# Grouped-query q norm folded into the exponentials' scale, with scalar maxima, first PSUM banks and the final scale changed

## The chip, the cores and the metric

The kernel runs on one core of a Trainium2 chip. The metric is the device time of one execution in microseconds (us), lower is better. The kernel before takes 1393.04 us, the median of three runs (1392.54 to 1395.71). Engine names as in the profile: PE is TensorE, DVE VectorE, ACT ScalarE, POOL GpSimd, SP SyncE, which issues the DMAs.

## The reference

Two layers of an encoder trunk over 512 tokens of 1024 features, f32, batch 1:

```
x = x + W_out [ NA-heads(h) || GQA-heads(h) ],   h = rms_norm(x) and one input projection
x = x + memory_cross_attention(rms_norm(x), rms_norm(mem))      4 heads of 128, 256 memory tokens
x = x + conv_ffn(rms_norm(x))                                   SwiGLU with a depthwise conv
return rms_norm(x)
```

The eight neighbourhood (NA) heads look at a window of the token grid. The grouped-query (GQA) part has 8 query heads and 2 key/value heads of 64, and this is what the change is mostly about:

```
g_q = apply_axial_rope(rms_norm(g_q, q_norm), cos, sin)      norm over each head's 64 numbers
g_k = apply_axial_rope(rms_norm(g_k, k_norm), cos, sin)
sc  = einsum('bqkgd,bskd->bkgqs', q, k) * HEAD_DIM ** -0.5
p   = softmax(sc);  o = p @ v
```

The rms of a query head is one number for a row of sc. So it can multiply q before the scores, or stand as a scale on the row of scores when its maximum is found and its exponentials are taken.

## The kernel before, in words

Activations lie transposed (features on partitions, 512 tokens along the row). Products in f32 precision are made from pairs of fp32r numbers, a high and a low part: each product is three matmuls (hi hi, hi lo, lo hi), so every tensor that PE reads has to be split: ACT casts (hi) and DVE or POOL subtracts (lo). Weights are loaded by SP, cast on ACT (L265) and subtracted on POOL (L266).

PE runs its instructions in the order of the program, and so does SP. The instructions of ACT, DVE and POOL are put in an order by a scheduler, by data and by priorities: `with behind(n)` makes instructions yield to others by n places, or go ahead where n is negative. `late(n, fn)` puts work off until n more units of PE's filler have been issued, so that its inputs are ready when PE comes to it.

PSUM has eight banks, in three pools: four "mm" (`ps_mm`, projections and attention values), two "sc" (`ps_s`, scores) and two "tr" (`ps_t`, transposes and small sums). A bank that is asked for again has to be read out first.

The stages of a layer. In attention the scores, softmax, transposes and values of 8 NA units and then of 16 GQA units of 128 queries (a pair of heads each) are woven step by step, and each step is filled up with other PE work worth some 2300 to 3000 ns, drawn from `attn_fill`. That is one sequence: the NA projections (`project_first` in layer 0, with the first three units interleaved; `project_qk`; `project_v`), the GQA projections in the order k, 0, 1, v, 2, 3 (`gqa_project`; 0 to 3 are q, two heads each), the NA part of the output projection (`out_na`), memory keys and values, and `close_rows`, the GQA part of the output projection. `attn_fill.step(N_FIRST ...)` runs the first units of it ahead of the weave. When the sequence has nothing ready, a step is not filled. Memory attention and the FFN follow.

The GQA path, `gqa_rope` (L834): q or k comes out of the projection in an mm bank `pm`. ACT writes xs, the bank by gain (L840), and its square sq (L841), DVE writes cc, the bank by gain and cosine (L842). Then pm is free. One unit later, `swap`: SP moves xs by 32 partitions into xr with four DMAs; PE sums sq over each head with the matrix `pairs`, into a tr bank; DVE makes v, mean square plus eps (L852, L855). Then `rotate`: POOL raises v to the power -1/2 (L862), copies it wide (L863), multiplies xr by the sine (L864) and adds cc (L865). Then `norm`: four PE matmuls with the identity turn the wide rows into a new mm bank (L77 `mm<-ident,t`). Then `split`: DVE multiplies (L875) and `split_q` (ACT L682, DVE L684) or `split_k` (ACT L664 and L666, DVE L668 and L670) makes the pairs. GQA's v goes through a transpose (`turn`).

The scores, `gqa_scores`: DVE takes each row's negative maximum out of the sc bank (L900), ACT the exponential with it as bias and the sum (L902); `gqa_normalise` takes 1/sum (L908) and multiplies (POOL L479). `normalise` (L478) is the tensor_scalar at L479, on DVE or POOL. NA's parts: scores L739, exponentials L745, one normalisation on ACT (L757), the others on POOL (L479), halves joined by L789 and L790, and the finished part split by `split_out` (ACT L499, POOL L500), which `out_na` waits for. `split_psum` is the general split (ACT L472, DVE L473).

Memory attention's scores, `mem_scores`: one DVE reduce for two query blocks (L1076), the product of the two maxima by 1/rms (L1077), two exponentials with 1/rms as scale (L1081). At the end of the kernel `scale` multiplies each half row of x by the final gain on ACT (L1241), beside the last residual adds (L1271) and the final norm (L400, L403, L413, L1249, L1251).

Line numbers in the text are those of the kernel before.

Of the kernel before, what the change touches and what calls it, by code (L numbers as in the profile page):

```python
# [10 lines left out]
F32 = mybir.dt.float32  # L11
F32R = mybir.dt.float32r
AF = mybir.ActivationFunctionType
ALU = mybir.AluOpType
# [4 lines left out]
P = 128  # L19
S = 512  # L20
# [29 lines left out]
MEM_FILL = [1, 1, 2, 2, 1, 3, 1, 3, 1, 3, 1]  # L50
N_ROWS = 3
MEM_STEPS = [0, 0, 1, 0, 1, 1, 1, 1, 1, 1, 1] + [0] * 9
W_BEHIND, N_RAW, N_W, AHEAD, AHEAD_HELD, N_WARM, N_LATE, N_FIRST = 45, 2, 4, 2, 5, 8, 4, 3


class InOrder:
# [117 lines left out]
def encoder_kernel(ctx: ExitStack, tc: tile.TileContext, t: dict, out: bass.AP):  # L174
# [29 lines left out]
    def rtile(shape, dt=F32R):  # L204
        return rpool.tile([P, *shape], dt, tag="r", name=nm("r"), padded_shape=[P, *pad(shape)])
# [63 lines left out]
    def get_w(key, ahead=AHEAD):  # L269
        n = done[0]  # L270
        assert plan[n][0] == key, (plan[n][0], key)
        ahead = n + 1 + ahead
        while ahead < min(len(plan), n + 1 + AHEAD_HELD) and plan[ahead][4][1:] == "r":
            ahead += 1
        while len(ready) < min(len(plan), ahead):
            while len(raws) < min(len(plan), len(ready) + N_RAW):
                emit_raw()
            emit_split()
        while len(raws) < min(len(plan), len(ready) + N_RAW):
            emit_raw()  # L280
        done[0] += 1
        w = ready[n]
        ready[n] = None
        return w
# [245 lines left out]

    mem_rstd = cpool.tile([P, MB], F32, name="mem_rstd")
    mem_rep = cpool.tile([P, MEMN], F32, name="mem_rep")

    def mem_stat():
        raw = load_mem()
# [53 lines left out]
    for l in range(DEPTH):  # L589
# [11 lines left out]
        def project_first():  # L601

            w, pms = {}, {}
            for u, k0, k1 in ((0, 0, 2), (1, 0, 2), (0, 2, 4), (1, 2, 4), (2, 0, 4), (0, 4, 6),
                              (1, 4, 6), (2, 4, 6), (0, 6, 8), (1, 6, 8), (2, 6, 8)):
                if u not in w:
                    w[u], pms[u] = get_w(NA_ORDER[u]), ps_mm()
                if (u, k0) == (0, 0):

                    for k in range(2):  # L610
                        PE.matmul(pms[u], w[u][0][:, k], xg[k][0], start=k == 0, stop=False)
                        PE.matmul(pms[u], w[u][0][:, k], xg[k][1], start=False, stop=False)
# [12 lines left out]

            late(1, evict)
            yield
# [2 lines left out]

        def project_qk(n, p):
            w = get_w((n, p))
            pm = ps_mm()
            gemm_T(pm, w, xg, range(0, 4), 0, KC - 1)
            yield
            gemm_T(pm, w, xg, range(4, 8), 0, KC - 1)
            if (n, p) == ("q", 0):
                mix.stat()
                held.append(pm)
            elif (n, p) == ("k", 0):  # L640
                mix.spread()
# [192 lines left out]

        def gqa_rope(g, pm):

            gain = qkg[:, l, 0:1] if g != "k" else qkg[:, l, 1:2]
            xs, sq, cc = tmp(), tmp(), tmp()
            with behind(-20):
                ACT.activation(xs, pm, AF.Copy, scale=gain)  # L840
                ACT.activation(sq, pm, AF.Square)  # L841
                DVE.scalar_tensor_tensor(cc, pm, gain, gtab[0][:, 0], op0=ALU.mult, op1=ALU.mult)  # L842

            def swap():
                xr = tmp()
                for i in range(4):
                    SP.dma_start(xr[32 * i : 32 * i + 32], xs[32 * (i ^ 1) : 32 * (i ^ 1) + 32])
                pv = ps_t()
                for b in range(NB):
                    PE.matmul(pv[:, 2 * b : 2 * b + 2], sq[:, b * P : (b + 1) * P], pairs, start=True, stop=True)  # L850
                v = small(2 * NB)
                DVE.tensor_tensor(v.rearrange("p (b j) -> p b j", j=2), pv[:, 0 : 2 * NB].rearrange("p (b j) -> p b j", j=2),  # L852
                                  r2[0].unsqueeze(2).to_broadcast([P, NB, 2]), op=ALU.mult)

                DVE.tensor_scalar(v, v, *((1.0 / HD, EPS) if g == "k" else (1.0, EPS * HD)), op0=ALU.mult, op1=ALU.add)  # L855
# [12 lines left out]
            def norm(xr, rows):  # L868
# [3 lines left out]
                late(1, lambda: split(xr, pr))  # L872

            def split(xr, pr):
                DVE.tensor_mul(pr, xr, pr)  # L875
                if g == "k":
                    gk.extend(rtile((2, S)) for _ in range(2))
                    split_k(pr, gk, False)
                else:
                    gq[g] = rtile((2, S))  # L880
                    split_q(pr, gq[g])

            late(1, swap)


        ga, gpt = {}, {}

        def gqa_scores(u):
            i, b = divmod(u, NB)
            qs = slice(b * P, b * P + P)  # L890
            assert gq[i] is not None and gk and gvt
            sc = [ps_s() for _ in range(2)]
            for j in range(2):
                for part in range(2):
                    PE.matmul(sc[j], gq[i][:, j, qs], gk[j][:, part], start=part == 0, stop=part == 1)
            nmx, sums = small(2), small(2)
            es = []
            for j in range(2):
                c = slice(j, j + 1)
                DVE.tensor_reduce(nmx[:, c], sc[j], axis=AX.X, op=ALU.max, negate=True)  # L900
                e = tmp()
                ACT.activation(e, sc[j], AF.Exp, bias=nmx[:, c], accum_out=sums[:, c])  # L902
                es.append(e)
            ga[u] = es, sums

# [114 lines left out]
        if l > 0:  # L1020
# [48 lines left out]
        def mem_scores(u):  # L1069
            h, bp = divmod(u, 2)  # L1070
            sc = ps_s().rearrange("p (i n) -> p i n", i=2)
            for i in range(2):
                qs = slice((2 * bp + i) * P, (2 * bp + i + 1) * P)
                mm3(sc[:, i, :], *(v[:, qs] for v in mqs[h]), *memk[h], True, True)
            nmx, sums = small(2), small(2)
            DVE.tensor_reduce(nmx, sc, axis=AX.X, op=ALU.max, negate=True)  # L1076
            DVE.tensor_mul(nmx, nmx, mq.rstd[:, 2 * bp : 2 * bp + 2])  # L1077
# [154 lines left out]
        def down_last(g):  # L1232
# [144 lines left out]
```

## Time and profile before

| | |
|---|---|
| median of three runs | 1393.04 us |
| the profiled execution | 1393.77 us |
| its span in the trace | 1392.0 us |
| mean granted clock of PE in it | 0.994 |
| instructions in the trace | 19198 |
| read from HBM, written | 125.00 MB, 2.10 MB |
| mean DMA rate | 91 GB/s over the span |

How to read it. The rows of the next section are from the page of the profile and from answers of its trace. A row in order of time has start, duration, engine, line, operation, out<-in, partitions x elements and type, and in brackets how long the engine was idle before it and what ended that. A group row has, after the bar, the busy time of all in us, the mean of one in ns, and the idle time before them. Rows of stretches have start:end, length, busy us (and count) of PE, of its weight load PEld, of DVE, ACT and POOL, then the mean granted clock, the DMA share and GB/s. A PE row's duration overlaps the next row's start, so the time that a matmul costs is read from start to start. A short group of several instructions is one row, with xN.

### The profile page before, as it was taken

Reading aid. Unit: us, or ns where it says so; the run is one execution under the profiler, and the core shown is the slowest. Engines: PE = TensorE matmul, PEld = TensorE weight load, DVE = VectorE, ACT = ScalarE, POOL = GpSimd, SP = SyncE. Lnnn points to the kernel's source line nnn. Section 1 sums busy time; section 2 is a strip of 40 time slices with the busy share of each in tenths; the row PEclk is TensorE's granted clock in tenths of the full one; section 3 lists DMA queues with packets and bytes.
Section 4 is the critical chain, followed back from the end, with each engine's and each line's share of the span. In section 5 each row is a group of like instructions: output and inputs, shape, how many; then the busy total and the mean of one; then the engine's idle time right before and its main releaser. Section 6 shows DMA issues by size and latency. Waiting matters only on the chain.

```text
span 1392.0 us, 19198 instructions
## 1 busy us (share of the span) xinstructions
PE 1354.7 (97%) x7072; PEld 1157.8 (83%) x7072; DVE 834.8 (60%) x1430; ACT 711.8 (51%) x1321; POOL 719.3 (52%) x537
## 2 busy tenths in 40 slices
PE   8999899999999999999999989999999999999997
PEld 7897789877888888888888978998788888888897
DVE  6666766364787177357446556754638843871873
ACT  6676577655443134234557656766554422432453
POOL 2458776635444444444645677756264444444441
PEclk9999999999999999999999999999999999999999
DMA  7653312422333333333356523223133333333331
GB/s 214 185 145 96 87 46 66 116 63 61 98 100 103 94 91 97 101 94 94 105 147 169 139 72 95 65 71 112 40 98 97 101 91 97 98 93 106 90 93 61
DMA packets 218205, 138.83 MB, mean 100 GB/s; under 512 B 6016, under 2 KB 211072, under 8 KB 218112
## 3 DMA queue, kind: packets, MB, share of 16 engines
q1 hardware_dynamic: 217968, 137.60, 34.6%
q8 instruction: 56, 0.92, 0.3%
q14 instruction: 37, 0.30, 0.1%
q10 hardware_dynamic: 144, 0.00, 0.0%
HBM read 125.00 MB, written 2.10 MB: 91 GB/s over the span
## 4 chain that ended last, share of the span: by engine, by line
PE 89%; DVE 4%; ACT 4%; issue 1%; DMA 1%; POOL 0%; DVEq 0%; ACTq 0%; SPq 0%
PE mm L77 82%; PE sc L77 4%; PE tr L64 3%; PE tr L77 1%; ACT hi L265 1%; DVE r L473 1%; DMA raw<-in_w_in 1%; ACT t L745 1%; DVE s L900 1%; DVE s L1077 1%; DVE xg L473 0%; DVE t L842 0%; ACT t L841 0%; ACT t L840 0%; ACT xg L438 0%
## 5 line engine op out<-in xcount | busy, mean ns | idle before, releaser
L266 POOL TENSOR_TENSOR lo<-raw,hi 128x1024 fp32r<-128x1024 f32 (+2 forms) x268 | 499.0, 1874 | 496.9 <-ACT hi L265 468.9
L77 PE MATMUL mm<-xg,hi 128*128 128x512 f32 x1984 | 617.7, 393 | 3.1 <-DVE t L842 2.9
L77 PEld LDWEIGHTS mm<-xg,hi 128*128 128x128 f32 x1984 | 370.4, 189 | 78.9 <-DVE t L842 3.3
L265 ACT CAST hi<-raw 128x512 fp32r<-128x512 f32 (+2 forms) x276 | 224.6, 837 | 346.7 <-PE mm L77 292.9
L77 PE MATMUL mm<-xg,lo 128*128 128x512 f32 x992 | 387.3, 391 | 0.0
L77 PE MATMUL mm<-r,hi 128*128 128x512 f32 (+1 forms) x1144 | 331.6, 374 | 2.3 <-ACT t L444 2.2
L77 PEld LDWEIGHTS mm<-r,hi 128*128 128x128 f32 x1144 | 207.3, 188 | 39.7 <-ACT t L444 3.1
L1201 DVE SCALAR_TENSOR_TENSOR t<-t,par,t 128x7 f32<-128x7 f32 (+1 forms) x352 | 201.9, 641 | 34.0 <-ACT t L1194 34.0
L77 PEld LDWEIGHTS mm<-xg,lo 128*128 128x128 f32 x992 | 187.1, 189 | 39.6
L77 PE MATMUL mm<-r,lo 128*128 128x512 f32 (+1 forms) x572 | 213.4, 373 | 0.0
L77 PEld LDWEIGHTS mm<-r,lo 128*128 128x128 f32 x572 | 108.0, 189 | 19.0
L1186 DVE TENSOR_TENSOR t<-mm,rep 128x512 f32<-128x512 f32 x88 | 60.1, 687 | 78.2 <-PE mm L77 62.1
L479 POOL TENSOR_SCALAR t<-t,s 128x512 f32<-128x512 f32 (+1 forms) x112 | 66.3, 608 | 75.4 <-DVE s L908 35.4
L1203 ACT ACTIVATE t<-t 128x512 f32<-128x512 f32 x44 | 27.8, 633 | 134.8 <-DVE t L1201 134.7
L1207 DVE TENSOR_TENSOR r<-t,r 128x512 fp32r<-128x512 f32 x44 | 90.5, 2056 | 7.4 <-ACT r L1206 4.3
L1230 DVE TENSOR_TENSOR xT<-xT,mm 128x512 f32<-128x512 f32 x32 | 21.9, 685 | 106.8 <-PE mm L77 106.8
L64 PE MATMUL tr<-ident,t 128*128 128x128 f32 x456 | 63.2, 275 | 13.3 <-DVE r L473 3.8
L77 PE MATMUL sc<-r,r 128*128 128x256 f32 (+1 forms) x352 | 72.6, 338 | 3.5 <-DVE r L473 2.5
L64 PEld LDWEIGHTS tr<-ident,t 128*128 128x128 f32 x456 | 52.4, 141 | 22.9 <-issue 9.7
L1194 ACT ACTIVATE t<-t,par 128x512 f32<-128x512 f32 x88 | 66.8, 806 | 3.2 <-DVE t L1186 3.2
L77 PE MATMUL mm<-r,r 128*128 128x256 f32 (+1 forms) x428 | 61.8, 297 | 0.0
L77 PEld LDWEIGHTS sc<-r,r 128*128 128x128 f32 x352 | 52.1, 192 | 8.3 <-DVE r L473 3.0
(145 smaller groups left out, 1554.1 us busy)
## 6 DMA issues: line engine op xcount, KB each, us to landing
raw<-in_w_up SPq DMA_DIRECT2D x88, 512.0 KB, 3.9
raw<-in_w_in SPq DMA_DIRECT2D x33, 512.0 KB, 4.5
raw<-in_w_down SPq DMA_DIRECT2D x32, 448.0 KB, 3.9
raw<-in_w_mem_kv SPq DMA_DIRECT2D x16, 512.0 KB, 4.0
raw<-in_w_down SPq DMA_DIRECT2D x16, 512.0 KB, 4.2
r<-in_bias SPq DMA_DIRECT2D x16, 384.0 KB, 5.8
r<-r SPq DMA_DIRECT2D x22, 256.0 KB, 5.2
raw<-in_w_out SPq DMA_DIRECT2D x8, 512.0 KB, 3.8
```

The source lines that it names most:

```text
L64: return lambda *a, **k: self.tc.keep_in_program_order(op(*a, **k))
L77: return self.tc.keep_in_program_order(self.engine.matmul(out, lhsT, rhs, **k))
L265: act.copy(hi[:, k], raw[:, k])
L266: (POOL if eng[0] == "P" else DVE).tensor_sub(lo[:, k], raw[:, k], f(hi)[:, k])
L473: DVE.tensor_sub(lo, ps, f(hi))
L479: eng.tensor_scalar(e, e, sums[:, col : col + 1], 1.0, op0=ALU.mult, op1=ALU.mult)
L1186: DVE.tensor_mul(u, us[side], ffn.rep)
L1194: ACT.activation(cc, u, AF.Identity, bias=par[:, l, CB + ch : CB + ch + 1], scale=w[1])
L1201: DVE.scalar_tensor_tensor(cc[:, dst], u[:, src], wi, cc[:, dst], op0=ALU.mult, op1=ALU.add)
L1203: ACT.activation(cs[0], cs[0], AF.Silu)
L1207: DVE.tensor_sub(acts[j][1], cs[0], f(acts[j][0]))
L1230: DVE.tensor_add(xT[m], xT[m], pm)
```

## The change

1. Fill ahead: N_FIRST is 4 instead of 3, so in layer 0 one more unit of the filler runs ahead of the weave; layer 1 keeps its 8 (3 + 5, now 4 + 4).
2. First banks: units 0 and 1 of `project_first`, and NA's q0 and k0 in `project_qk`, take a score bank instead of an mm bank.
3. q's head norm: q's cc is written in place in its bank pm. The four swap DMAs are issued right after xs, for k as well. For q there is no wide copy, no POOL addition and no matmul with the identity: POOL's power is kept in `qr[g]` at low priority (behind 40), DVE adds the rotated part into pm, and `split_q` reads pm. k keeps its norm, made in `expand` and `norm`.
4. `gqa_scores`: the negative maximum is multiplied by qr in a 128x1 tensor_scalar on DVE for each head, and qr is the scale of the exponential.
5. `mem_scores`: the 128x2 product is two 128x1 tensor_scalars.
6. The final scale is a tensor_scalar on DVE, without a priority, instead of an ACT activation behind 20.

Counted over the two layers, the mm<-ident matmuls go from 40 to 8 instructions, DVE gets 96 small products more (64 in `gqa_scores`, 32 in `mem_scores`, for 16 removed) and the 16 final scales, ACT has 16 instructions fewer, POOL 16 fewer, and SP's number is the same.

```diff
-... N_LATE, N_FIRST = 45, 2, 4, 2, 5, 8, 4, 3
+... N_LATE, N_FIRST = 45, 2, 4, 2, 5, 8, 4, 4
...
+    qr = [cpool.tile([P, 2 * NB], F32, name=f"qr{i}") for i in range(4)]
...
-                    w[u], pms[u] = get_w(NA_ORDER[u]), ps_mm()
+                    w[u], pms[u] = get_w(NA_ORDER[u]), ps_s() if u < 2 else ps_mm()
...
         def project_qk(n, p):
-            pm = ps_mm()
+            pm = ps_mm() if p else ps_s()
...
         def gqa_rope(g, pm):
-            xs, sq, cc = tmp(), tmp(), tmp()
+            xs, sq, xr = tmp(), tmp(), tmp()
+            cc = tmp() if g == "k" else pm
...
-            def swap():
-                xr = tmp()
-                for i in range(4):
-                    SP.dma_start(xr[32 * i : 32 * i + 32], xs[32 * (i ^ 1) : 32 * (i ^ 1) + 32])
+            for i in range(4):
+                SP.dma_start(xr[32 * i : 32 * i + 32], xs[32 * (i ^ 1) : 32 * (i ^ 1) + 32])
+
+            def rotate():
                 pv = ps_t()
...
-                late(1, lambda: rotate(xr, v))
-
-            def rotate(xr, v):
-                r = small(2 * NB)
-                rows = tmp()
+                POOL.tensor_mul(xr, xr, gtab[0][:, 1])
+                if g == "k":
+                    POOL.tensor_add(xr, cc, xr)
+                    late(1, lambda: expand(v))
+                else:
+                    with behind(40):
+                        POOL.tensor_tensor(qr[g], v, mhalf[:, : 2 * NB], op=ALU.pow)
+                    late(1, add)
+
+            def add():
+                DVE.tensor_add(pm, pm, xr)
+                gq[g] = rtile((2, S))
+                split_q(pm, gq[g])
+
+            def expand(v):
+                r, rows = small(2 * NB), tmp()
                 with behind(-40):
                     POOL.tensor_tensor(r, v, mhalf[:, : 2 * NB], op=ALU.pow)
                     POOL.tensor_copy(rows.rearrange(...), r.unsqueeze(2).to_broadcast([P, 2 * NB, HD]))
-                POOL.tensor_mul(xr, xr, gtab[0][:, 1])
-                POOL.tensor_add(xr, cc, xr)
-                late(2, lambda: norm(xr, rows))
+                late(2, lambda: norm(rows))
...
-            late(1, swap)
+            late(1, rotate)
...
         def gqa_scores(u):
                 DVE.tensor_reduce(nmx[:, c], sc[j], axis=AX.X, op=ALU.max, negate=True)
+                normalise(nmx[:, c], qr[i], r)
-                ACT.activation(e, sc[j], AF.Exp, bias=nmx[:, c], accum_out=sums[:, c])
+                ACT.activation(e, sc[j], AF.Exp, bias=nmx[:, c], scale=qr[i][:, r : r + 1], accum_out=sums[:, c])
...
-        attn_fill.step(N_FIRST if l == 0 else N_FIRST + 5)
+        attn_fill.step(N_FIRST if l == 0 else N_FIRST + 4)
...
         def mem_scores(u):
-            DVE.tensor_mul(nmx, nmx, mq.rstd[:, 2 * bp : 2 * bp + 2])
+            for i in range(2):
+                normalise(nmx[:, i : i + 1], mq.rstd, 2 * bp + i)
...
             def scale(half, m):
-                with behind(20):
-                    ACT.activation(xc, xc, AF.Copy, scale=gfin[:, m : m + 1])
+                DVE.tensor_scalar(xc, xc, gfin[:, m : m + 1], 1.0, op0=ALU.mult, op1=ALU.mult)
```

The body of `norm` and `split`, shortened here, stays for k; the scale of q's score (1/8) is in v's constants as before.

More of the change, by code (lines that the diff above doesn't have):

```diff
@@ L52 @@
 MEM_STEPS = [0, 0, 1, 0, 1, 1, 1, 1, 1, 1, 1] + [0] * 9
-W_BEHIND, N_RAW, N_W, AHEAD, AHEAD_HELD, N_WARM, N_LATE, N_FIRST = 45, 2, 4, 2, 5, 8, 4, 3
+W_BEHIND, N_RAW, N_W, AHEAD, AHEAD_HELD, N_WARM, N_LATE, N_FIRST = 45, 2, 4, 2, 5, 8, 4, 4
 class InOrder:
@@ L863, in rotate, with norm @@
                     POOL.tensor_copy(rows.rearrange("p (b d) -> p b d", d=HD), r.unsqueeze(2).to_broadcast([P, 2 * NB, HD]))
-                POOL.tensor_mul(xr, xr, gtab[0][:, 1])
-                POOL.tensor_add(xr, cc, xr)
-                late(2, lambda: norm(xr, rows))
-            def norm(xr, rows):
+                late(2, lambda: norm(rows))
+            def norm(rows):
                 pr = ps_mm()
@@ L871, in norm, with split @@
                     PE.matmul(pr[:, b * P : (b + 1) * P], rows[:, b * P : (b + 1) * P], ident, start=True, stop=True)
[L872 to L876, printed above, removed]
+                def split():
+                    DVE.tensor_mul(pr, xr, pr)
                     gk.extend(rtile((2, S)) for _ in range(2))
                     split_k(pr, gk, False)
-                else:
-                    gq[g] = rtile((2, S))
-                    split_q(pr, gq[g])
-            late(1, swap)
+                late(1, split)
+            late(1, rotate)
         ga, gpt = {}, {}
@@ L899, in gqa_scores @@
                 c = slice(j, j + 1)
+                r = 2 * b + j
                 DVE.tensor_reduce(nmx[:, c], sc[j], axis=AX.X, op=ALU.max, negate=True)
+                normalise(nmx[:, c], qr[i], r)
                 e = tmp()
-                ACT.activation(e, sc[j], AF.Exp, bias=nmx[:, c], accum_out=sums[:, c])
+                ACT.activation(e, sc[j], AF.Exp, bias=nmx[:, c], scale=qr[i][:, r : r + 1], accum_out=sums[:, c])
                 es.append(e)
```

## The prediction

> **What bounds the kernel now.** I read the page's busy shares first, then the chain that ended last, then the list of what TensorE (PE) waited for, and last the order in time around each of its gaps.
>
> ```profile
> span 1392.0 us, 19198 instructions
> PE 1354.7 (97%) x7072; PEld 1157.8 (83%) x7072; DVE 834.8 (60%) x1430; ACT 711.8 (51%) x1321; POOL 719.3 (52%) x537
> ...
> PE 89%; DVE 4%; ACT 4%; issue 1%; DMA 1%; POOL 0%; DVEq 0%; ACTq 0%; SPq 0%
> ```
>
> PE is busy for 97% of the span and makes 89% of the chain. The other engines have 40% and more to spare, so an instruction saved on them counts only at a gap of PE. Three things can move the time: PE instructions that go, PE gaps that open or close, and the clock that PE is granted. The gaps, from the list of waits of PE over the whole run (total, times, longest):
>
> ```profile
> PE tr L64 <- DVE r L473: 3.8, 2, 1.9
> PE mm L77 <- DVE t L842: 2.9, 2, 1.4
> PE tr L77 <- ACT t L841: 2.7, 2, 1.3
> PE sc L77 <- DVE r L473: 2.5, 2, 1.3
> PE tr L64 <- DVE t L479: 2.5, 4, 0.8
> PE tr L64 <- DVE xg L473: 2.3, 2, 1.7
> ...
> PE tr L64 <- DVE s L908: 1.8, 2, 0.9
> PE tr L64 <- POOL r L524: 1.7, 1, 1.7
> PE mm L77 <- DVE r L684: 1.5, 1, 1.5
> ...
> PE tr L64 <- ACT mem_rep L555: 0.8, 1, 0.8
> PE sc L77 <- ACT t L902: 0.7, 1, 0.7
> PE sc L77 <- DVE r L670: 0.3, 1, 0.3
> ```
>
> Most rows come twice, once for each layer, and most of them lie in the GQA projection, which is where the change works. The clock, in stretches of 8 us (PEclk is the number before the DMA share):
>
> ```profile
> 148.00:156.00 8.00, 7.09 (x32) 6.22 (x33) 3.92 (x9) 3.75 (x9) 8.00 (x9) 0.79 0.62 177
> 820.00:828.00 8.00, 6.09 (x30) 5.05 (x28) 4.71 (x7) 4.20 (x8) 5.06 (x4) 0.79 0.25 69
> 834.00:842.00 8.00, 7.04 (x32) 6.17 (x33) 3.92 (x9) 3.78 (x9) 8.00 (x10) 0.79 0.60 176
> ```
>
> Each of these holds one gap (the 1.9 of L473 in layer 1, the 1.3 of L841 in both layers) and each loses 0.21 x 8 = 1.7 us of full clock. So a stall can have a price beside its length; I don't take it that every stall has.
>
> **The change part by part.** The terms are against the profiled execution (1393.77 us: its span and 1.8 around it), 0.73 above the median of the three runs, 1393.04.
>
> *q's head norm, what goes.* For each q unit four multiplications with the identity go; in both layers that is 8 of the 10 norms. Two groups of instructions, then two pieces in order of time:
>
> ```profile
> L77 PE MATMUL mm<-ident,t 128*128 128x128 f32 x80 | 12.2, 303 | 0.0
> ...
> L875 DVE TENSOR_TENSOR mm<-t,mm 128x512 f32<-128x512 f32 x10 | 7.0, 696 | 11.8 <-PE mm L77 10.5 <-POOL r L524 0.7 <-issue 0.7
> ```
>
> ```profile
> 116.66 1.05 PE L77 MATMUL mm<-ident,t 128*128 128x128 f32 x8
> 117.46 1.20 PE L77 MATMUL mm<-r,r 128*128 128x256 f32 x8
> ```
>
> The group's 80 records are 8 to a norm. The next matmul starts 117.46 - 116.66 = 0.80 us after a norm's first (the 1.05 overlaps it), so 8 norms are **-6.4 us**. POOL also loses a copy and an addition for each q. Nothing waits there that is not counted below, so these are 0; were POOL's cover gone, they could only gain.
>
> *q's head norm, what comes.* q's projection bank used to be read once by three instructions and was then free. Now the rotated q is made in it, and it is free only after the addition, ACT's two casts and DVE's two subtractions. There are four such banks, and in the changed order the next users are v and the NA values. In layer 1, around the old gap of L842:
>
> ```profile
> 803.55 0.54 ACT L757 ACTIVATE t<-t,s 128x256 f32<-128x256 f32 x1
> 803.95 1.18 ACT L664 CAST r<-mm 64x512 fp32r<-64x512 f32 x2
> 804.54 0.73 PE L77 MATMUL mm<-xg,hi 128*128 128x512 f32 x2 [1.44 <-DVE t L842]
> 805.16 1.41 DVE L668 TENSOR_TENSOR r<-mm,r 64x512 fp32r<-64x512 f32 x2 [0.68 <-ACT r L664]
> ```
>
> After the change ACT's order here is the two reads of q1, NA's L757, then q0's casts (1.17) and only then k's casts (1.18, at 803.95 before). From 804.2 (NA's L757 with a handover), q0's casts end at 805.4, k's at 806.6; DVE's subtractions (1.41 a pair) end at 806.5 for q0 and 807.95 for k. v takes k's bank: it starts at 808.0 instead of 804.54, **+3.5 us**. The turn of v in layer 1 (1.9 before) then waits for what the 0.80 of q1's norm hid: **+0.7**.
>
> In layer 0 the same banks meet other users. The two NA value steps after q1 wait for q0's split and k's split: NA's L757 0.54 + casts 1.18 + subtractions 1.41 is some 3.1 after ACT's reads, with k's pair behind it about 3.3 of stall in all, against 1.4 at v before: **+1.9**. q3's square sums come right behind q3's matmuls, and ACT reads q3 only after q2's casts (addition 0.70 at L875's size and casts 1.18): about 3.2 against 1.3: **+1.9**. What the added unit ahead (N_FIRST 4) moves: the output projection out_na now starts before the last NA part is split, whose cast stands behind q3's casts on ACT, and POOL's subtraction behind that:
>
> ```profile
> 146.00 0.62 ACT L499 CAST r<-t 128x512 fp32r<-128x512 f32 x1 [1.32 <-DVE t L791]
> ...
> 146.69 1.28 POOL L500 TENSOR_TENSOR r<-t,r 128x512 fp32r<-128x512 f32 x1 [1.61 <-PE mm L77]
> ```
>
> Addition 0.70, casts 1.18, 0.62 and 1.28 are 3.8, with handovers **+4.1**. Smaller ones, at k's square sums: **+0.6**. These are estimates from rows followed through the changed order; a lower end is that engines catch up and half of the 12.7 us of this paragraph and the last is not seen, an upper end a quarter more.
>
> *What the same order closes.* The turn of v in layer 0 falls behind other PE work: **-1.9**. In layer 0 the gaps of L524 1.7, L902 0.7, L473 (xg) 0.7 and mem_rep 0.8 stand in work that now comes after the pause at out_na: 3.9 becomes about 0.5, **-3.4**. In layer 1 the 1.7 of L473 (xg) stood behind q's subtractions on DVE, which are done earlier: **-1.7**.
>
> *First banks.* Units 0 and 1 of the first projection and NA's q0 and k0 take score banks, so v's first blocks have mm banks and no longer wait for q0's split (L684 1.5) and the first scores not for k's (L670 0.3): **-1.8**. The bounds are 0 (scores wait for their own banks) and -1.8; I take -1.8, as two blocks of v now lie between.
>
> *Scalar maxima.* Memory attention multiplies 128x2 maxima by 1/rms, with two operands in SBUF (L1077). Two of eight in each layer take ten times as long; DVE and POOL, in order of time:
>
> ```profile
> 112.60 1.28 POOL L266 TENSOR_TENSOR lo<-raw,hi 128x512 fp32r<-128x512 f32 x1
> 113.35 0.55 DVE L855 TENSOR_SCALAR s<-s 128x8 f32<-128x8 f32 x1
> ...
> 282.56 4.77 POOL L266 TENSOR_TENSOR lo<-raw,hi 128x1024 fp32r<-128x1024 f32 x2 [1.18 <-ACT hi L265]
> 285.88 1.47 DVE L1077 TENSOR_TENSOR s<-s,s 128x2 f32<-128x2 f32 x1
> ...
> 293.06 2.40 POOL L266 TENSOR_TENSOR lo<-raw,hi 128x1024 fp32r<-128x1024 f32 x1 [5.73 <-ACT hi L265]
> 295.27 0.61 DVE L479 TENSOR_SCALAR t<-t,s 128x256 f32<-128x256 f32 x2
> ...
> 302.64 2.38 POOL L266 TENSOR_TENSOR lo<-raw,hi 128x1024 fp32r<-128x1024 f32 x1 [7.18 <-ACT hi L265]
> 303.13 1.91 DVE L1077 TENSOR_TENSOR s<-s,s 128x2 f32<-128x2 f32 x1
> ```
>
> Both slow L1077 end 0.02 us after POOL's subtraction (287.35 to 287.33, 305.04 to 305.02): DVE was held. The PE gaps L479 0.8 and L473 1.3 of each layer come right behind. The new form is that of L479, whose pair ran through the end of a POOL subtraction (295.46) at 0.61. So the hold goes: -2 x (0.76 + 1.27) = -4.1; the 16 more small instructions, 0.16 each by L400's row below, are hidden but for the unfilled ones, +0.3: **-3.8**. But L855, a one-input operation with fixed numbers, ends 113.90 beside POOL's 113.88: held too. That is a rival below.
>
> The Trainium skill, "SBUF — State Buffer", section "Who interferes with whom", has it that DVE with two SBUF inputs contends with a GpSimd operation that reads SBUF, and that a tensor_scalar in a two-port mode does so as well. The trace agrees on L1077 and on L855; L479, a tensor_scalar, doesn't show it, so by the rule taken strictly the sum would be 3.8 higher, by the row it stands.
>
> *Exponentials' scale.* 64 more small products on DVE and a scale for each Exp. In filled steps PE has other work. Where the fill has run out, the gap of L908 (0.9, once a layer) grows to about 1.2; in layer 0 the added unit ahead spends fill earlier, so a second step is unfilled: **+1.8** in both layers (0.3 + 0.3 + 1.2). Bounds 0 and twice that.
>
> *Final scale.* One row of DVE in the tail:
>
> ```profile
> 1383.70 0.16 DVE L400 TENSOR_SCALAR s<-tr 128x2 f32<-128x2 f32 x1 [1.37 <-PE tr L77]
> ```
>
> The scale goes from ACT to DVE, in DVE's idle 1.37 before L400: 0, at most one instruction of about 0.35, some half of L479's pair.
>
> *Clock.* The new stalls of more than 3 us come one to a layer more than the ones they replace: 2 x 1.7 = **+3.4**. Bounds -5.1 (the three stretches go) and +6.8.
>
> The Trainium skill, "TensorE: Matmul & The Clock Gate", section "What's actually happening", puts the half rate at an idle window of about 3.4 us; by that alone stalls of 1.3 and 1.9 would cost nothing, but the rows above show three that do.
>
> **Sum.** Goes: 6.4 + 1.9 + 3.4 + 1.7 + 1.8 + 3.8 = 19.0. Comes: 3.5 + 0.7 + 1.9 + 1.9 + 4.1 + 0.6 + 1.8 + 3.4 = 17.9. Net -1.1 on the execution, and from the median 1393.04 about **1392.0 us**.
>
> **The rivals.**
> - *Faster: the banks come free in time.* If q0's addition runs before q1's reads are due, v starts near its old time (-3.5), q3's sums and out_na wait no more than before (-6.0), and no stretch is added (-3.4): 1392.0 - 12.9 = 1379; with half of it 1385.5. For: ACT 51% and DVE 60% busy; the swap is issued earlier. Against: ACT is in order, and its casts stand behind others. Some of it is likely; I give it 1386.
> - *Slower: q's held bank.* One mechanism: PE finds no free bank from k to q3, because split_q stands behind another head's reads on ACT. If q2 and q3 in layer 1 stall as in layer 0 (+1.9 and +1.9) and the clock drops once more (+1.7), the time is 1397.5. It decides once a wait at v, at the NA values or at q3's sums is over 4 us. For: four banks, three heads at once.
> - *The hold stays* (tensor_scalar held as L855 was): +3.8, 1395.8. For: L855. Against: L479.
> - *The change doesn't do what it says:* PE's identities hid a wait, so their 6.4 turn into gaps: 1392.0 + 6.4 = 1398.4. The row shows it for q1 (its 0.80 is inside the turn's wait), for others not.
>
> **How the numbers follow.** Forecast near 1392.0: 0.36. Faster rival 0.32. Held banks 0.20, hold stays 0.06, identities hidden 0.06. What a measurement of this kernel can tell from no change is about 0.2%, 2.8 us: 1390.3 to 1395.8. Half of the cases of "hold stays" fall within. Faster 0.34, same 0.37, slower 0.29. The forecast's own range is 1389.5 to 1395; the range of 8 in 10, from most of the faster rival to both slower ones, is 1384 to 1399.
>
> **What would show it.** mm<-ident records 16 instead of 80; no L685 wait at v's first blocks; memory attention without gaps of 1.27 and with each small product under 0.2; v in layer 1 starting some 3.5 later after k's norm; a wait of about 4 at out_na in layer 0; five half-clock stretches rather than three. Waits at v and out_na under 2 would make the prediction wrong on the fast side; a third stall of over 3 us in a layer, on the slow side.

## The result, and the profile after

The changed kernel takes 1414.64 us, the median of four runs (1411.82 to 1415.72), against 1392.79 for the kernel before beside it (1392.32 to 1395.71): a ratio of 1.0146 with a 95% interval of 1.013 to 1.0162. The medians are 21.9 us apart. The prediction said 1392.0 with a range of 1384 to 1399, and was wrong.

The page of the changed kernel, the lines that answer to those shown of before:

```profile
span 1410.0 us, 19114 instructions
PE 1359.9 (96%) x7008; PEld 1156.3 (82%) x7008; DVE 845.0 (60%) x1526; ACT 708.5 (50%) x1305; POOL 706.3 (50%) x521
...
PE 86%; DVE 5%; ACT 4%; DMA 2%; issue 1%; POOL 1%; SPq 0%; DVEq 0%; ACTq 0%; POOLq 0%
```

PE has 64 instructions' records fewer and yet is busy for 5.2 us longer; its share of the chain falls from 89% to 86%. What it waited for over the whole run, the rows over 2.5 us and the one for DMAs:

```profile
PE mm L77 <- DVE r L685: 6.6, 3, 4.0
PE tr L64 <- DVE xg L473: 4.5, 3, 2.1
PE tr L77 <- ACT t L844: 4.2, 2, 2.9
PE mm L77 <- POOL r L492: 3.9, 2, 1.9
PE tr L64 <- POOL t L479: 2.9, 1, 2.9
PE tr L64 <- DVE r L473: 2.8, 1, 2.8
...
PE mm L77 <- DMA r<-r: 2.2, 1, 2.2
```

All rows of the full list add up to 42.6 us, those of before to 30.1: 12.5 more. The busy PE that does less work is the clock. Stretches of 8 us with PEclk ahead of the DMA share:

```profile
120.00:128.00 8.00, 6.15 (x19) 5.05 (x20) 6.20 (x9) 3.96 (x8) 3.55 (x4) 0.57 0.61 187
...
796.00:804.00 8.00, 6.14 (x18) 5.01 (x19) 2.82 (x10) 3.73 (x12) 6.28 (x7) 0.57 0.51 141
816.00:824.00 8.00, 5.94 (x16) 4.69 (x17) 5.25 (x8) 2.57 (x5) 2.20 (x2) 0.57 0.77 220
```

0.79 in such a row is one half-clock stretch (1.7 us lost), 0.57 is two on end (3.4). The mean granted clock of the whole span is 0.985 against 0.994, so 0.015 x 1410 - 0.006 x 1392 = 12.8 us more are lost. Together: waits 12.5, clock 12.8, less the identities' 6.4 us of work, is 18.9 for a span that is 18.0 longer. These three account for it.

Where it lies, by one gap of PE that both kernels have at the end of each layer's memory attention, first before and then after:

```profile
327.01 0.73 PE L77 MATMUL mm<-r,hi 128*128 128x512 f32 x2 [1.12 <-ACT t L444]
...
1008.61 0.73 PE L77 MATMUL mm<-r,hi 128*128 128x512 f32 x2 [1.12 <-ACT t L444]
```

```profile
333.06 0.73 PE L77 MATMUL mm<-r,hi 128*128 128x512 f32 x2 [1.12 <-ACT t L444]
...
1026.03 0.73 PE L77 MATMUL mm<-r,hi 128*128 128x512 f32 x2 [1.12 <-ACT t L444]
```

6.0 us come up to the first of these gaps and 11.4 more up to the second, though memory attention itself got shorter. The new stops lie in attention; the FFN of layer 0, between the two gaps, lost nothing (the same weight load of layer 1, below, is issued at 778.02 before and at 784.10 after, 6.1 later).

### The profile page after: what moved, and what is told of

Same layout as the page of the kernel before. It is cut to its first block, busy times and chain, and to the rows that moved or that the text cites. A ratio compares the mean times of both kernels' runs of the same rounds, so it can differ in the third digit from the quotient of the medians.

```text
span 1410.0 us, 19114 instructions
## 1 busy us (share of the span) xinstructions
PE 1359.9 (96%) x7008; PEld 1156.3 (82%) x7008; DVE 845.0 (60%) x1526; ACT 708.5 (50%) x1305; POOL 706.3 (50%) x521
## 4 chain that ended last, share of the span: by engine, by line
PE 86%; DVE 5%; ACT 4%; DMA 2%; issue 1%; POOL 1%; SPq 0%; DVEq 0%; ACTq 0%; POOLq 0%
PE mm L77 77%; PE sc L77 4%; PE tr L64 3%; PE tr L77 1%; ACT hi L265 1%; DVE s L909 1%; DMA raw<-in_w_in 1%; POOL lo L266 1%; DVE xg L473 0%; DMA xT<-in_xT 0%; ACT t L912 0%; ACT r L683 0%; DVE r L685 0%; DVE t L455 0%; ACT t L746 0%
## 5 line engine op out<-in xcount | busy, mean ns | idle before, releaser
L77 PE MATMUL mm<-xg,hi 128*128 128x512 f32 x1920 | 598.3, 393 | 0.2 <-DVE r L669 0.2
L77 PEld LDWEIGHTS mm<-xg,hi 128*128 128x128 f32 x1920 | 359.6, 189 | 72.8 <-PE mm L77 0.5
L77 PE MATMUL mm<-xg,lo 128*128 128x512 f32 x960 | 375.6, 391 | 0.0
L77 PEld LDWEIGHTS mm<-xg,lo 128*128 128x128 f32 x960 | 181.6, 189 | 38.7
L1241 DVE TENSOR_TENSOR xT<-xT,mm 128x512 f32<-128x512 f32 x32 | 21.9, 685 | 106.8 <-PE mm L77 106.8
L77 PE MATMUL mm<-r,r 128*128 128x256 f32 (+1 forms) x428 | 65.7, 306 | 9.0 <-DVE r L685 6.2
L77 PEld LDWEIGHTS mm<-r,r 128*128 128x128 f32 x428 | 58.4, 198 | 12.4 <-ACT r L665 4.2
```

Source lines behind the costliest of these rows:

```text
L77: return self.tc.keep_in_program_order(self.engine.matmul(out, lhsT, rhs, **k))
L1241: DVE.tensor_add(xT[m], xT[m], pm)
```

## The experiments

The first theory (A) was the prediction's own slow rival with more weight: q's held bank and the swap DMAs ahead of others stop PE, and each stop may bring a half-clock stretch. The rival (B) put the time on the fill ahead and the first banks, which move the order of the layer. Ratios are to the kernel before, on the same chip.

**q_alone.** Only the q norm part of the change; the rest is put back, here against the changed kernel:

```diff
-... N_LATE, N_FIRST = 45, 2, 4, 2, 5, 8, 4, 4
+... N_LATE, N_FIRST = 45, 2, 4, 2, 5, 8, 4, 3
...
-                    w[u], pms[u] = get_w(NA_ORDER[u]), ps_s() if u < 2 else ps_mm()
+                    w[u], pms[u] = get_w(NA_ORDER[u]), ps_mm()
...
-                normalise(nmx[:, i : i + 1], mq.rstd, 2 * bp + i)
+            DVE.tensor_mul(nmx, nmx, mq.rstd[:, 2 * bp : 2 * bp + 2])
...
-                DVE.tensor_scalar(xc, xc, gfin[:, m : m + 1], 1.0, op0=ALU.mult, op1=ALU.mult)
+                    ACT.activation(xc, xc, AF.Copy, scale=gfin[:, m : m + 1])
```

> The kernel before with q's norm as the exponentials' scale alone (held bank, swap DMAs early); fill ahead, first banks, scalar maxima and final scale as before. Theory A (q's held bank and the swap DMAs ahead of others in SP's queue make PE stalls, and each stall of some 2 us or more a half-clock stretch): 20 to 28 us slower than before, about 1415 to 1420, with at least five half-clock stretches between 100 and 900 us. Theory B (the added fill unit and the first banks disturb the order of the layer): within 5 us of before.

Measured 1428.64, ratio 1.0263 (1.0249 to 1.0277): 36.6 slower than before. Above A's range, and B is out: the loss is in the q norm. Alone it is worse than with the others. In layer 0 PE waits 3.73 for the DMAs that build NA's v, a wait that the changed kernel doesn't have there (which of the other changes hides it wasn't tested):

```profile
109.50 1.72 PE L77 MATMUL mm<-r,r 128*128 128x256 f32 x6 [3.73 <-DMA r<-r]
```

**others.** The complement: fill ahead, first banks, scalar maxima and final scale, with q's norm as it was before. The edit is the diff of the change without `gqa_rope`, `gqa_scores` and `qr`.

> The kernel before with fill ahead, first banks, scalar maxima and final scale, without q's norm change. Theory A: about 5 us faster than before (memory attention's gaps of 2.0 us a layer and what follows them), some 1387 to 1389. Theory B: 10 to 25 us slower than before.

Measured 1385.67, ratio 0.9956 (0.9942 to 0.9969): 6.4 faster. It is faster than the kernel before and than the changed kernel.

**swap_late.** The changed kernel, with the swap DMAs and POOL's product (now in `turned`, with q's power) each one unit later, where they stood before:

```diff
-            for i in range(4):
-                SP.dma_start(xr[...], xs[...])
             def rotate():
+                for i in range(4):
+                    SP.dma_start(xr[...], xs[...])
...
+                late(1, lambda: turned(v))
```

> The changed kernel with the four swap DMAs and POOL's product put off as they were before. If the swap in SP's queue, ahead of the five DMAs that NA's values wait for in layer 1, costs a stall of 2.2 us and two half-clock stretches of 1.7 there: some 4 to 6 us faster than the changed kernel, about 1409. If the queue doesn't matter: the same as the changed kernel or slower, as q is ready later.

Measured 1412.06, ratio 1.0138 (1.0124 to 1.0152), not apart from the changed kernel's 1.0146; the 4 to 6 us that were expected aren't seen. The wait for the DMAs is gone, but all stops of PE in its trace add up to 45.4, against 42.6 in the changed kernel: others took its place. That the queue holds is plain in the traces. SP's issues in layer 1 of the kernel before, and then of the changed one:

```profile
778.02 0.39 SPq L64 DMA_DIRECT2D raw<-in_w_in  x1
778.50 3.37 SPq L64 DMA_DIRECT2D r<-r  x5
...
785.28 2.46 SPq L64 DMA_DIRECT2D t<-t  x4
```

```profile
784.10 0.39 SPq L64 DMA_DIRECT2D raw<-in_w_in  x1
791.36 2.46 SPq L64 DMA_DIRECT2D t<-t  x4
793.92 3.12 SPq L64 DMA_DIRECT2D r<-r  x5
...
797.86 1.87 PE L77 MATMUL mm<-r,r 128*128 128x256 f32 x6 [2.18 <-DMA r<-r]
```

SP stood for 6.9 us with nothing issued, because the swap (t<-t) waits for ACT's read of q's bank and everything behind it in the queue waits too. The five DMAs (r<-r) that NA's values need were issued 15.4 us later than before, 6.0 of which layer 0 had lost already, and PE stopped for 2.18 and then ran at half clock (796 to 804 above).

**q_free.** q's bank free after three reads, a new bank for the sum:

```diff
-            cc = tmp() if g == "k" else pm
+            cc = tmp()
...
-                DVE.tensor_add(pm, pm, xr)
-                split_q(pm, gq[g])
+                pr = ps_mm()
+                DVE.tensor_add(pr, cc, xr)
+                split_q(pr, gq[g])
```

> The changed kernel, but q's cosine part goes to SBUF as before, so that q's projection bank is free after three reads; the addition writes into a new bank just before the split. Norm in the scale as changed. Theory A: the stalls at the NA values (4.0 in layer 1, 2.2 in layer 0) and their half-clock stretches go, 8 to 14 us faster than the changed kernel, about 1402 to 1406. If the split's place on ACT and not the held bank is what counts: within 3 us of the changed kernel.

Measured 1416.81, ratio 1.0173 (1.0152 to 1.0195): no faster than the changed kernel. Where the changed kernel stops for 4.03 and 0.25 in layer 1 (rows in the next section), q_free has:

```profile
815.23 0.74 PE L77 MATMUL mm<-r,r 128*128 128x256 f32 x4 [1.85 <-DVE t L845]
816.91 1.22 PE L77 MATMUL mm<-xg,hi 128*128 128x512 f32 x2 [0.94 <-DVE r L685]
```

That is 1.5 less at this place. But the stops of the whole trace add up to 42.4 against the changed kernel's 42.6, so theory A fell as far as the total goes. The second theory (C) was the place of q's split: it stands three fill units earlier than before and meets k's split and the next head's reads on ACT and DVE. Its rival (D) was the exponentials' scale.

**q_free_later.** q_free with q's addition and split three units later:

```diff
-                    late(1, add)
+                    late(4, add)
```

> q_free with q's addition and split put off by three more fill units, to where the split stood before; swap DMAs early. Theory C (it is the place of q's split that costs: two units behind the projection it meets k's split and the next head's reads on ACT and DVE, and PE waits for both): 10 to 20 us faster than q_free, some 1397 to 1406. Theory D (the 3 units don't matter; exponentials' scale, fill and clock cost the time): within 4 us of q_free's 1417.

Measured 1408.49, ratio 1.0125 (1.0109 to 1.0142): 8.3 us less than q_free, short of C's 10 to 20 and more than D's 4. At the place just shown one stop of 1.37 is left, about that of before (1.44).

**q_later.** The same edit on the changed kernel, so that the projection bank is held for the three units.

> The changed kernel, q's projection bank held, with the addition and split put off by three more fill units. Theory C: some 8 to 15 us faster than the changed kernel. Theory A (a held bank costs): slower than the changed kernel by 5 us or more, as each bank is held for three more units.

Measured 1417.97, ratio 1.0194 (1.0176 to 1.0213): slower than the changed kernel, and 9.5 us slower than q_free_later. So a held bank does cost where the split is late. Where the split is early, it makes no difference that can be told.

**q_paced.** Free bank, and swap, product, rotation and split at the units where they stood before (q_free and swap_late together, with `late(3, add)`). What is left of the q change is that identities, wide copy and one POOL addition are gone, and that the scale is in the exponentials.

> Free bank, and swap, rotation and split all at the units where they stood before; only the four identity matmuls, the wide copy and one POOL addition of each q are gone, and the scale is in the exponentials. Theory C: the identities' 6.4 us are gained on the 1386 of the kernel with the other changes alone, less the scale's price: 1380 to 1388. Theory D: 1400 or more.

Measured 1398.52, ratio 1.0054 (1.0039 to 1.0069). C's 1380 to 1388 isn't had, and D's 1400 is missed by 1.5. Against q_free_later only the swap and POOL's product (with q's power) are at their old place: 10.0 us. Most of it is clock: the mean granted clock of the runs is 0.992 against 0.987, some 8 us, while the stops in the two traces add up to 37.8 against 38.7. One part is tied to the DMA queue. In q_free_later PE waits 2.20 for the five DMAs of layer 1, as in the changed kernel, and 3.4 us of clock are lost right behind it:

```profile
794.00:802.00 8.00, 6.65 (x19) 5.36 (x20) 2.28 (x6) 3.81 (x12) 5.75 (x7) 0.57 0.46 131
```

q_paced has neither. The rest is stretches elsewhere, some behind stops that both have: v's turn stops for 2.80 in q_free_later and 2.79 in q_paced, and only the first lost 1.7. q_paced is still 13 above the others' kernel.

**exp_scale.** The others' kernel with the products and the scale put in, all with a scale of one:

```diff
                 DVE.tensor_reduce(nmx[:, c], sc[j], axis=AX.X, op=ALU.max, negate=True)
+                normalise(nmx[:, c], one8, r)
-                ACT.activation(e, sc[j], AF.Exp, bias=nmx[:, c], accum_out=sums[:, c])
+                ACT.activation(e, sc[j], AF.Exp, bias=nmx[:, c], scale=one8[:, r : r + 1], accum_out=sums[:, c])
```

> The kernel with the other changes alone (fill ahead, first banks, scalar maxima, final scale; q's norm as before), with the 64 small products and the exponentials' scale put in with a scale of one. Theory C: within 2 us of that kernel's 1386 (a gap of 0.9 grows to 1.0 to 1.2). Theory D: 8 us slower or more, with new gaps behind the GQA scores.

Measured 1398.9, ratio 1.0053 (1.004 to 1.0065): 13.2 us slower than the others' kernel. C's 2 us fall and D holds for this part, with nothing moved in the projection at all. One step in layer 0 of exp_scale:

```profile
197.18 0.69 DVE L903 TENSOR_REDUCE s<-sc 128x1 f32<-128x512 f32 x1
197.90 0.69 DVE L473 TENSOR_TENSOR xg<-tr,xg 128x512 fp32r<-128x512 f32 x1
198.51 0.68 DVE L903 TENSOR_REDUCE s<-sc 128x1 f32<-128x512 f32 x1
199.11 0.68 DVE L473 TENSOR_TENSOR xg<-tr,xg 128x512 fp32r<-128x512 f32 x1
199.70 0.33 DVE L479 TENSOR_SCALAR s<-s,one 128x1 f32<-128x1 f32 x2
...
200.69 0.78 ACT L906 ACTIVATE t<-sc,s,one 128x512 f32<-128x512 f32 x1
...
201.61 1.50 PE L77 MATMUL sc<-r,r 128*128 128x512 f32 x4 [1.05 <-ACT t L906]
```

The same step in the others' kernel:

```profile
196.64 0.69 DVE L900 TENSOR_REDUCE s<-sc 128x1 f32<-128x512 f32 x1 [0.65 <-PE sc L77]
...
197.43 0.69 ACT L902 ACTIVATE t<-sc,s 128x512 f32<-128x512 f32 x1 [0.24 <-DVE s L900]
```

Without the product, the exponential starts 0.10 after its maximum is done (197.33). With it, the maximum is done at 197.87 and its product, 0.2 us long, comes at 199.70, behind two evictions of transposes (L473) and the other head's maximum in DVE's order. Then ACT has other casts ahead. The exponential starts 2.8 us after its maximum. Over all 64, the mean time from the end of a maximum to the start of its exponential is 0.37 in the others' kernel, 1.65 in exp_scale and 1.65 in the changed kernel. The exponential is the last reader of its score bank, there are two such banks, and the next scores wait on PE (1.05).

**exp_only.** exp_scale without the products (scale of one as an operand, 64 times):

> The kernel of the other changes with the exponentials' scale (of one) alone, without the 64 small products. Theory E (the small product costs: it comes behind a PSUM eviction on DVE and holds both exponentials back): some 1387 to 1389, as each exponential is 0.08 us longer and nothing else moves. Theory F (the scale as an operand costs by itself): 1395 or more.

Measured 1385.87, ratio 0.9958 (0.9942 to 0.9974): the others' kernel to 0.2 us. Theory E holds and F falls: the scale is free, although each exponential takes longer, as the groups of exp_only show against the 0.69 above:

```profile
L905 ACT ACTIVATE t<-sc,s,one 128x512 f32<-128x512 f32 x64 | 49.8, 782 | 19.4 <-DVE s L903 19.1 <-DVE s L911 0.2
```

**exp_act.** exp_scale with each product on ACT, right ahead of its exponential:

```diff
-                normalise(nmx[:, c], one8, r)
+                ACT.activation(nmx[:, c], nmx[:, c], AF.Copy, scale=one8[:, r : r + 1])
```

> exp_scale (scale of one) with the 64 small products on ACT, right before their exponentials, and not on DVE. Theory E: DVE's order is as without them, and the cost is some 0.2 us of ACT a product: 1388 to 1393. Theory F: as exp_scale, 1396 to 1400.

Measured 1390.52, ratio 0.9994 (0.9983 to 1.0004). 8.4 of the 13 us are gone, with the same arithmetic, and the mean time from maximum to exponential is 0.92: most of the cost is having the product on DVE. The run takes its 0.2 us off DVE as well as its place in the order; the rows above, where it comes 1.8 after its maximum, point at the place, but the run doesn't part the two. The products take 0.29 each on ACT, and the 4.7 us left were not taken apart.

**q_paced_act.** q_paced with the products on ACT.

> q_paced (free bank, everything at the units of before, identities gone) with the small products on ACT. Theory E: as much faster than q_paced's 1398.5 as exp_act is than exp_scale, 1388 to 1393. If the DVE order is not what costs there: 1396 to 1400.

Measured 1396.9, ratio 1.0034 (1.002 to 1.0047). E's gain isn't had here: only 1.6 us, though the maximum is followed sooner here too (0.78 against 1.59). In the traces the stops of PE are 4.6 shorter in all (33.2 against 37.8), but the mean clock of the runs is 0.9905 against 0.9923, some 2.5 us more lost. What is worth 8.4 with identities is not worth it without them, and why stays open.

**clock_fill.** The changed kernel with 16 useless matmuls in layer 1, where PE waits 4.03 for q0's split:

```diff
+                if l == 1:
+                    idle = ps_t()
+                    for _ in range(16):
+                        tc.keep_in_program_order(nc.tensor.matmul(idle, xg[0][0][:, 0:P], xg[0][0], start=True, stop=True))
```

> The changed kernel with 16 matmuls without use in layer 1, right behind k's norm, where PE waits 4.0 us for q0's split; they are not counted as fill, so nothing else is moved. Theory G (a PE pause brings the half clock): the two half-clock stretches at 816 to 824 us (3.4 us lost) are gone, and the time is some 3 us shorter than the changed kernel, though PE does more. If the clock falls for another reason: they stay, and the time is the same or longer.

Measured 1414.71, ratio 1.0169 (1.0147 to 1.019): the same as the changed kernel; the 3 us forecast are not seen. Three stretches of clock_fill:

```profile
816.00:824.00 8.00, 6.89 (x38) 5.74 (x37) 5.54 (x9) 6.86 (x17) 5.49 (x7) 1.00 0.33 93
840.00:848.00 8.00, 6.88 (x33) 5.96 (x34) 4.47 (x8) 2.81 (x6) 1.72 (x2) 0.79 0.34 98
954.00:962.00 8.00, 5.90 (x25) 4.64 (x24) 2.94 (x6) 4.14 (x8) 5.66 (x5) 0.79 0.25 75
```

At its place the trace fits theory G: 1.00 where the changed kernel has 0.57. The total didn't follow. In the changed kernel's profile the stop of 2.79 at v's turn and the two of 1.95 at L492 were not followed by a half clock; here stops of 2.80 and 1.95 at the same places were. So the same stop is followed by a stretch in one execution and not in another, and for that reason the 1.00 of one execution is no proof that the filling kept the clock.

The Trainium skill, "TensorE: Matmul & The Clock Gate", section "What's actually happening", lets a free-running window of some 3.4 us decide, so that a stop's place against it would count. That fits this, but no run here shows the window itself. The stops of 1.3 and 1.9 that lost 1.7 us are shorter than the whole idle window of its table; there the measurement decides.

The third question was why 6.4 us of identities gave nothing. Theory H: they hid waits. Theory R: something else in q_paced costs as much.

**q_paced_pe.** q_paced with the four identity matmuls put back at their old place, written into the bank that the addition then overwrites:

```diff
+            def waste():
+                pr = ps_mm()
+                for b in range(NB):
+                    PE.matmul(pr[...], cc[:, b * P : (b + 1) * P], ident, start=True, stop=True)
+                late(1, lambda: add(pr))
```

> q_paced with q's four identity matmuls put back at their old place, as work without use (their bank is overwritten by the addition). Theory H (the identities hid waits; without them the same waits are PE gaps): within 3 us of q_paced's 1398.5. Theory R (they are PE time like any other, and something else of q_paced costs 6): 1404 to 1406.

Measured 1398.68, ratio 1.0049 (1.0035 to 1.0062): 0.2 from q_paced. Theory H is shown. All stops of PE add up to 37.8 in the trace of q_paced and to 31.4 in that of q_paced_pe: 6.4 less, for 8 x 0.80 of work put back. One of them is the turn of v, here in layer 1 of q_paced and then of q_paced_pe:

```profile
822.38 0.63 PE L64 MATMUL tr<-ident,t 128*128 128x128 f32 x4 [2.79 <-DVE r L473]
```

```profile
826.84 0.63 PE L64 MATMUL tr<-ident,t 128*128 128x128 f32 x4 [1.96 <-DVE r L473]
```

0.83 less wait with 0.80 more work.

**q_noscale.** q_paced without product, scale and power: q's norm is left out of the computation.

> q_paced without q's norm altogether: no product, no scale, no power; q goes into the scores unnormalised. It leaves the norm of q out. Theory H: no gain against the kernel with the other changes alone, 1384 to 1389, though 8 x 0.80 us of PE work is gone. Theory R: 1378 to 1381.

Measured 1388.48, ratio 0.9978 (0.9965 to 0.999): 2.8 above the others' kernel with 6.4 us less PE work. H again: in this order of the units even a norm for nothing would not have paid.

**mem_only.** The kernel before with the scalar maxima alone.

> The kernel before with the scalar maxima of memory attention alone. If the held product is all behind memory attention's gaps: 4 to 5.5 us faster than before, about 1386 to 1388, by two gaps of 0.76 and two of 1.27 and part of the two of 0.49. If the one-input form is held as well: within 1 us of before.

Measured 1387.38, ratio 0.9966 (0.9953 to 0.998): 4.3 faster. Two rows of it, the small product beside POOL's subtraction; of the three gaps in layer 0 one of 0.32 is left:

```profile
301.29 2.40 POOL L266 TENSOR_TENSOR lo<-raw,hi 128x1024 fp32r<-128x1024 f32 x1 [7.21 <-ACT hi L265]
301.78 0.21 DVE L479 TENSOR_SCALAR s<-s,s 128x1 f32<-128x1 f32 x1
```

**first_only.** The kernel before with the fill ahead and the first banks alone.

> The kernel before with the fill ahead and the first banks alone. By the prediction's terms 1.8 us faster than before (the gaps of 1.51 and 0.27 go), plus or minus one half-clock stretch of 1.7: 1388 to 1391. If the order of the whole of layer 0 moves: up to 5 us either way.

Measured 1390.38, ratio 0.9987 (0.9977 to 0.9997): 1.3 faster.

## Why the prediction was wrong

By the steps of the prediction, and with the medians of the kernels one after the other:

| step | predicted | measured |
|---|---|---|
| scalar maxima | -3.8 | -4.3 (mem_only) |
| first banks | -1.8 | -1.3 (first_only) |
| all of the others, final scale too | -5.6 | -6.4 (others) |
| exponentials' products | +1.8 | +13.2 (exp_scale) |
| identities | -6.4 | 0 (q_paced_pe, q_paced) |
| swap DMAs and POOL's product one unit ahead | no term | +10.0 (q_free_later over q_paced) |
| split three units earlier | part of 12.7 | +8.3 (q_free over q_free_later) |
| held bank | part of 12.7 | about -2, not apart from 0 (changed kernel over q_free) |
| clock | +3.4 | +12.8 (traces; contained in the rows above) |

The rows but the last lead from the kernel before to the changed one: -6.4 + 13.2 - 0.4 + 10.0 + 8.3 - 2.2 = 22.5, against 21.9 measured. The order of the steps matters (q_alone shows that the parts are not independent), so this is one path and not the price of each.

*What bounds the kernel* was right: gaps, work and clock of PE make the whole difference. In these three terms the prediction for the profiled execution was -6.4 of work, +1.9 of waits and +3.4 of clock. The trace of the changed kernel has those matmuls gone, +12.5 of waits and +12.8 of clock. So the work that goes was right as work; the waits and the clock are what it had wrong, by some 10 us each. *Scalar maxima* and *first banks* were right in mechanism and size. The product in its new form isn't held by POOL (0.21 inside POOL's 2.40); the rival that the hold stays is out.

*Exponentials' scale* failed as a step. "In filled steps PE has other work" took for granted that the product follows its maximum at once. In the step shown it came 1.8 us later, because DVE's order puts other ready work between, and the two score banks carry the delay to PE. The term was bounded by twice 1.8; the run showed 13.2.

*q's head norm, what goes* failed: 6.4 us of PE work were counted as time, and they hid waits of the same size, which now stand as stops (q_paced_pe). That was the prediction's last rival, at 0.06.

*What comes* was right where it was worked from rows. v in layer 1, which takes k's bank, was predicted to start 3.5 later after k's norm (mm<-ident). In the kernel before v starts at 804.54 (row in the prediction), 3.45 after this one:

```profile
801.09 1.05 PE L77 MATMUL mm<-ident,t 128*128 128x128 f32 x8
```

In the changed kernel it starts 6.99 after it, so 3.54 later:

```profile
812.26 1.05 PE L77 MATMUL mm<-ident,t 128*128 128x128 f32 x8
...
815.07 1.18 ACT L683 CAST r<-mm 64x512 fp32r<-64x512 f32 x2
816.27 1.19 ACT L665 CAST r<-mm 64x512 fp32r<-64x512 f32 x2
816.27 1.39 DVE L685 TENSOR_TENSOR r<-mm,r 64x512 fp32r<-64x512 f32 x2 [0.68 <-ACT r L683]
817.70 1.41 DVE L669 TENSOR_TENSOR r<-mm,r 64x512 fp32r<-64x512 f32 x2
817.81 1.19 PE L77 MATMUL mm<-r,r 128*128 128x256 f32 x4 [4.03 <-DVE r L685]
819.25 1.19 PE L77 MATMUL mm<-xg,hi 128*128 128x512 f32 x2 [0.25 <-DVE r L669]
```

The 4.03 stands at the NA values (mm<-r,r), which wait for q0's split, and 0.25 at v. The other stops that the prediction named came as well, mostly somewhat shorter: at the NA values of layer 0 2.17 and 0.31 (3.3 predicted), at q3's sums 2.94 (3.2), at out_na 1.87 and 0.86 (4.1), at the turn of v in layer 1 2.79 (2.6).

The chain of casts and subtractions is the one of the prediction. But the held bank, by which the prediction named it, is not what decides the time: with the bank free (q_free) this place is shorter and the total the same, and with a free bank and the split three units later the total is 8.3 shorter. So the place of the split is what the runs show to cost; that it costs by meeting k's split on ACT and DVE is read from the rows above.

*The swap* had no term. The prediction named SP's queue nowhere, and counted the earlier swap for the faster rival, though the swap is an instruction that waits and five DMAs that PE needs stood behind it. The rows show 2.18 of stop and 3.4 of clock for this in layer 1. The 10.0 of the table holds POOL's product and more clock beside it, and on the changed kernel the same step back gains only 2.6 (swap_late), so the full price of the queue stays open.

*What the same order closes* was wrong by some 7 us in waits. The turn of v in layer 0 did close. But the layer 1 wait of L473 (xg), 1.7 before, became 2.1 and not 0, and the waits after out_na in layer 0, 3.9 before and 0.5 predicted, were traded for others of 5.8. Both layers also got a wait of 1.95 at L492, for which there was no term; the others' kernel has one of the two already.

*Clock* was mis-sized: +12.8 where +3.4 was taken and +6.8 was the bound, some seven more half-clock stretches than before where two were expected. It was priced by stalls of over 3 us, but the trace has one such stall only (4.03), and its stretches also follow stops of 1.3 to 2.9.

## What to carry to other kernels

A small instruction in the middle of a chain across engines can cost its place in the queue of its engine, and not just its 0.2 us (64 of them 13.2 us here). Measure the chain with a neutral operand, and try it on the engine that reads its result: that gained 8.4 us in one kernel here and 1.6 in another. Work taken off the busiest engine is worth its time only where no wait stands behind it; putting it back as useless work shows that in one run. A DMA that waits for a computation holds everything behind it in its queue, so list what is behind before moving it up.

## What was not expected of the hardware

In these traces the half clock comes in pieces of 1.7 us lost, after stops from 1.3 us, and not after each: a stop of 1.95 at the same place lost nothing in the changed kernel and 1.7 in clock_fill. Where a stop of 4.03 was filled with useless matmuls the one trace has a clock of 1.00, against 0.57 unfilled. An exponential with a scale from SBUF takes 0.78 instead of 0.69 for 128x512, and costs nothing in this kernel.
